# A hybrid attention and RWKV-7 layer: scratch regrouped by four pairs, initial states turned up front

## The chip, the cores and the metric

The kernel runs on one core of one Trainium2 chip. The metric is the device time of one execution in microseconds. A core has five engines with rows of instructions of their own: TensorE (PE, matmuls and transposes), VectorE (DVE), ScalarE (ACT), GpSimd (POOL) and SyncE (SP), which here issues nearly all transfers; 16 DMA engines carry them out. On-chip tiles have 128 partitions.

## What is computed

One inference step of one layer for 256 prompt tokens and 1024 latent tokens of width 1024. One input projection feeds two groups, whose gated outputs go through one output projection:

```python
u = h @ w_in
q, k, v, g_a, u_b, g_b = split(u)
# (A) differential attention, 8 heads of 2 x 64; latent tokens also read 512 cached keys
s = einsum('bqhmd,bkhmd->bhmqk', q, k) * scale
p = softmax(s)
a = p[:, :, 0] - lam * p[:, :, 1]
o_a = rmsnorm(einsum('bhqk,bkhv->bqhv', a, v), subln_g) * (1 - lam_init) * silu(g_a)
# (B) RWKV-7, 16 heads of 64, both directions; r, w, k, v, kk, b come from u_b
def step(S, inp):
    sa = einsum('bhvk,bhk->bhv', S, -kk_t)
    S = S * w_t + sa[..., None] * b_t + v_t[..., None] * k_t
    return S, einsum('bhvk,bhk->bhv', S, r_t)
# prompt: S starts at 0, its final S is an output; latent: S starts at state_rwkv
x = x + gate * (concat([o_a, o_b]) @ w_out)
y = rmsnorm(x, final_g)
```

Outputs are y of both kinds of tokens, the new keys and values of the prompt, and the prompt's final RWKV states (new_s).

## The kernel before

Everything is float32; a projection matmul is done in three passes, the operands split into a high part (hi) and a remainder (lo). The 16 RWKV heads are taken as 8 pairs p of two heads h; d is the direction.

**Projections (0 to about 1223 us).** The 66 weight blocks of 128 columns are taken in a fixed plan. For each, `load_w` (L161) loads the block into one tile w, `split_w` (L167, L170) makes whi and wlo one block ahead of its use, and `chunk` (L337 to L339) runs 24 matmuls for each of three token ranges into a PSUM tile psg. Behind every chunk, the generators of earlier blocks are taken one step on: `b_qk` (L578) makes rotated queries and keys of an attention head, `b_k`/`products`/`gram` the matrices kt, bt, ra of an RWKV pair, and so on. Results go to scratch in DRAM by `spill` (L379), issued on SP: q and k each as two arrays, hi and lo, with one row of 1280 or 1792 tokens for each of 1024 channels. In `b_qk` of a key head the cached keys leave first (L608, L609; 256 KB each), then hi in three pieces through one tile "hi" (L624 to L627), then lo as one store of 640 KB; the last two heads store hi in one piece.

**Mix (from about 1223 us).** The recurrence runs 10 items (two groups of four pairs, each with the prompt and four segments of 256 tokens) of 8 steps (ticks) of 32 tokens, both directions at once; two steps are a part j. `load_part` (L770) brings a part's operands to slots L and R, `load_early` (L792) Bt and Tb for the part after next. `step` (L920) does: 32 matmuls into bank 0 (L933) and their copy into R (L940, ACT), attention work by `fill(0)`, 32 matmuls into bank 1 (L951) and the multiply by the decay on DVE that makes the next state (L962), 32 matmuls for y (L975), the products of Tb and Bt for the next part (`prep` L812, into yb, then `put` L818 on ACT), and more attention by `fill(1)`. PE takes its row in order; the row is made by the tile scheduler from the order of the code, with the step's matmuls raised in priority. `start_item` (L882) turns the states by 64x64 transposes in bank 1 where the prompt's item ends and the latent one begins (L895 to L899). `store_y` (L996), `norm`, `attention` (`load_q` L1064, `load_k` L1072) and `project` (L1309) do the rest; `inverse` (L725) makes Tb's source for each item on POOL.

Names: P = 128, HD = 64, CH = 32 (tokens of a step), HN = 2 (steps of a part), NL = 4 (pairs of a group), T = 1280, NK = 1792, D = 1024.

## Time and profile before

| what | us |
|---|---|
| median of three runs | 2551.7 (2549.16 to 2551.72) |
| the profiled execution | 2542.46 |
| its span | 2540.3 |
| PE busy in the span | 2299.6 (91%) |
| DVE, ACT, POOL busy | 1491.8, 1222.8, 1149.4 |

The profile is of one execution. Its span runs from the first to the last recorded instruction. Busy shares are means over the whole span, and the two halves of the kernel differ much; where a stage is meant, the windows of that stage are read. A DMA share is a mean over 16 engines. [...]

### The profile page before, as it was taken

The numbers are of one execution on the slowest core, as the hardware profiler recorded it, in microseconds if no ns is written. First come the engines' busy times: TensorE is split into PE (matmuls) and PEld (weight loads), VectorE is DVE, ScalarE is ACT, GpSimd is POOL, SyncE is SP. The second block draws the span as 40 slices with busy tenths as digits, with TensorE's granted clock in tenths as the row PEclk, the third lists the DMA queues.
The fourth block names the chain that finished last, engine by engine and source line by source line (L and its number), as shares of the span: only waits on it lengthen the run. The fifth ranks groups of instructions, "written<-read, shape, count | busy, mean of one in ns | idle before, by whom it ended". The sixth has DMA issues, their size and how long they took to land.

```text
span 2540.3 us, 60748 instructions
## 1 busy us (share of the span) xinstructions
PE 2299.6 (91%) x23907; PEld 1880.0 (74%) x23907; DVE 1491.8 (59%) x2950; ACT 1222.8 (48%) x2528; POOL 1149.4 (45%) x1665
## 2 busy tenths in 40 slices
PE   5999999999999999999578887999898889897886
PEld 4888888888888888887467676767686677675675
DVE  5665574646555755433347675666665564666676
ACT  3333444343433444332366676667566565553353
POOL 4244244352433443447554764457485121133274
PEclk9999999999999999999689898999999899998998
DMA  7455656566655565665998897786879889767435
GB/s 246 111 153 135 185 146 171 142 167 164 156 138 160 144 162 138 163 168 158 240 183 166 188 188 167 160 181 148 191 176 224 221 205 223 178 182 217 141 122 183
DMA packets 544893, 437.59 MB, mean 172 GB/s; under 512 B 182151, under 2 KB 481331, under 8 KB 542048
## 3 DMA queue, kind: packets, MB, share of 16 engines
q1 hardware_dynamic: 542512, 427.96, 66.8%
q0 software_dynamic: 2096, 5.75, 1.2%
q8 instruction: 189, 3.10, 0.5%
q14 instruction: 96, 0.79, 0.1%
HBM read 258.69 MB, written 163.86 MB: 166 GB/s over the span
## 4 chain that ended last, share of the span: by engine, by line
PE 53%; DMA 14%; POOL 9%; DVE 8%; SPq 6%; ACT 5%; issue 4%; POOLq 0%; DVEq 0%; ACTq 0%
PE sc L1099 4%; PE po L1144 4%; PE pg L452 3%; PE bank L951 3%; PE pa L1129 2%; PE yb L812 2%; DMA yn<-y 1%; PE pso L1352 1%; PE ptk L456 1%; PE bank L975 1%; PE bank L933 1%; PE psg_v L338 1%; ACT pb L1107 1%; PE psg_v L339 1%; PE psg_v L337 1%
## 5 line engine op out<-in xcount | busy, mean ns | idle before, releaser
L1099 PE MATMUL sc<-ka,q 128*128 128x512 f32 (+1 forms) x832 | 296.0, 447 | 40.1 <-DVE pb L1102 34.3
L1107 ACT ACTIVATE pb<-pb,mn 128x1536 f32<-128x1536 f32 (+1 forms) x160 | 218.3, 1365 | 97.8 <-DVE pb L1102 94.7
L1102 DVE TENSOR_SCALAR_CACHE_REDUCE pb<-sc,mn 128x512 f32<-128x512 f32 x256 | 191.5, 748 | 113.1 <-PE sc L1099 104.8
L1144 PE MATMUL po<-vk,aT 128*128 128x128 f32 x1600 | 233.6, 287 | 3.7 <-ACT aT L1131 3.6
L1144 PEld LDWEIGHTS po<-vk,aT 128*128 128x128 f32 x1600 | 212.9, 198 | 22.7 <-ACT aT L1131 5.7
L484 POOL TENSOR_SCALAR ta<-ta,ka 128x256 f32<-128x256 f32 x80 | 93.8, 1172 | 291.3 <-DVE bk L482 287.0
L738 POOL TENSOR_TENSOR tmp<-aw,tt 128x31 f32<-128x31 f32 (+15 forms) x310 | 165.5, 534 | 120.3 <-DMA aw<-bt 40.0
L459 ACT COPY km<-ptk 64x256 f32<-64x256 f32 x320 | 117.6, 367 | 209.5 <-PE ptk L456 169.8
L1099 PEld LDWEIGHTS sc<-ka,q 128*128 128x128 f32 x832 | 142.1, 202 | 81.7 <-DVE pb L1102 53.1
L740 POOL TENSOR_TENSOR tt<-tt,tmp 128x31 f32<-128x31 f32 (+15 forms) x310 | 183.3, 591 | 19.9
L962 DVE TENSOR_TENSOR R<-bank,wc 64x256 f32<-64x256 f32 x312 | 131.0, 420 | 76.4 <-PE bank L951 73.0
L818 ACT COPY L<-yb 32x384 f32<-32x384 f32 x312 | 146.6, 470 | 56.6 <-PE yb L812 52.8
L453 DVE TENSOR_TENSOR km<-pg,msk 128x512 f32<-128x512 f32 x80 | 55.2, 690 | 200.2 <-PE pg L452 188.4
L1121 DVE SCALAR_TENSOR_TENSOR pb<-pb,cc,pb 128x512 f32<-128x512 f32 (+1 forms) x208 | 170.6, 867 | 2.0
L1102 DVE TENSOR_SCALAR_CACHE_REDUCE pb<-sc 128x512 f32<-128x512 f32 (+1 forms) x160 | 101.3, 635 | 87.0 <-PE sc L1099 72.8
L1129 PE MATMUL pa<-ident,pb 128*128 128x128 f32 x800 | 135.1, 287 | 14.1 <-DVE acc L1346 9.0
L1131 ACT COPY aT<-pa 128x512 f32<-128x512 f32 (+1 forms) x208 | 115.1, 570 | 64.4 <-PE pa L1129 62.3
L940 ACT COPY R<-bank 32x256 f32<-32x256 f32 x320 | 116.1, 363 | 54.1 <-PE bank L933 49.9
L951 PEld LDWEIGHTS bank<-R,L 128*64 128x64 f32 x2560 | 91.9, 150 | 56.4 <-ACT R L940 36.1
L951 PE MATMUL bank<-R,L 128*64 128x64 f32 x2560 | 105.0, 239 | 29.3 <-ACT R L940 29.0
L1129 PEld LDWEIGHTS pa<-ident,pb 128*128 128x128 f32 x800 | 97.9, 145 | 43.6 <-DVE acc L1346 11.6
L1336 POOL TENSOR_TENSOR olo<-of,ohi 128x512 fp32r<-128x512 f32 x30 | 39.0, 1298 | 195.6 <-ACT ohi L1335 120.9
(354 smaller groups left out, 6388.2 us busy)
## 6 DMA issues: line engine op xcount, KB each, us to landing
acc<-acc SPq DMA_DIRECT2D x50, 512.0 KB
ra<-ra SPq DMA_DIRECT2D x160, 128.0 KB
kt<-km SPq DMA_DIRECT2D x160, 128.0 KB
bt<-km SPq DMA_DIRECT2D x160, 128.0 KB
Bt<-bt SPq DMA_DIRECT2D x80, 256.0 KB
L<-kt SPq DMA_DIRECT2D x80, 256.0 KB
L<-ra SPq DMA_DIRECT2D x80, 256.0 KB
R<-vb SPq DMA_DIRECT2D x160, 64.0 KB
```

What stands on the lines that cost most here:

```text
L459: nc.scalar.copy(km[64 * h:64 * h + 64, e:NC:2, 0:HD], pt[64 * e:64 * e + 64, :, 64 * h:64 * h + 64])
L738: e.tensor_tensor(mv, aw[:n, t, t + 1:CH].unsqueeze(2).broadcast_to([n, w, j]), tt[:n, t:t + 1, 0:j].broadcast_to([n, w, j]), op=ALU.mult)
L740: e.tensor_tensor(tt[:n, t + 1:CH, 0:j], tt[:n, t + 1:CH, 0:j], mv, op=ALU.add)
L818: nc.scalar.copy(L[96:128, :, q // 2, q % 2, :, 0:96], pp[32 * q:32 * q + 32, 0:192 * HN].rearrange("p (e c y) -> p e c y", e=2, y=96))
L951: x = nc.tensor.matmul(bank[1][hv(h), o_:o_ + 64], L[:, e, h, d, k, 0:64], R[:, k, d, e, hv(h)], start=True, stop=True, tile_position=(0, ...
L962: hold(nc.vector.tensor_tensor(dst[:, :, :, hv(h)], bank[1][hv(h), 256 * w:256 * w + 256].rearrange("p (d e v) -> p d e v", e=2, d=2), wcs ...
L1099: nc.tensor.matmul(sc, q[:, v, m, qc], ka[:, m, 0:kn], start=(v == 0), stop=(v == 1))
L1102: nc.vector.tensor_scalar(pm[:, c * 512:c * 512 + kn], sc, -0.125, mn[:, c - 1:c] if c else None, op0=ALU.mult, op1=ALU.min, accum_out=mn[ ...
L1107: soon.append(lambda: nc.scalar.activation(v, v, AF.Exp, bias=mn[:, c:c + 1], scale=-1.0, accum_out=B["l"][:, m, B["b"]:B["b"] + 1]))
L1121: nc.vector.scalar_tensor_tensor(a, B["p"][1][:, v], B["cc"], a, op0=ALU.mult, op1=ALU.add)
L1129: nc.tensor.transpose(pt[:, t * P:(t + 1) * P], B["p"][0][:, 512 * c + t * P:512 * c + (t + 1) * P], ident)
L1144: nc.tensor.matmul(po, B["aT"][c][:, t * P:(t + 1) * P], vk[:, t, :], start=(c == 0 and t == 0), stop=(c == last and t == nt - 1))
```

## The change

- The scratch of q becomes one array [H, HD, 2, 2, T] and that of k [H, 2, HD, 2, NK], with hi/lo and the two 64-channel halves as dimensions of their own. The loads of q go from 4 transfers a tile to 2 (64 rows of 4 pieces), those of k from 2 to 1. The stores keep their number; on the DRAM side they are now walked as 2 halves by 64 rows (`r m t -> m r t`).
- ra, kt and bt are grouped by four pairs, not two; a slot has one L and one R, Bt and Tb one tile each. load_part goes from 8 transfers to 4; load_early from 6 to 2, and is issued once in a part, in its second step, behind the second prep and its put; this prep itself moves from behind the y matmuls to behind the first 32 matmuls of that step.
- All initial states are loaded, transposed (16 transposes of 128x64) and stored to scratch s0 among the last projections, and loaded from there at an item's head; the prompt's final state gets a tile of its own, fin, and is turned and stored in the next tick (`new_state`). start_item and load_pairs go.
- The decay multiply is two instructions of 64x512 in place of four of 64x256; the columns of bank 1 are ordered by direction first.
- The rows of oT are reordered so that project loads one tile in one transfer.

SP issues 1827 transfers in place of 2282; DVE has 2378 instructions in place of 2534, ACT 2254 for 2264, PE 16107 for 16139.

SP's row at the first q tile of the projections (hiq is the high part, uq the remainder, km the tile of kt and bt). Before:

```order
77 L379 DMA qhi<-hiq_0_1993 128x512
78 L379 DMA qhi<-hiq_512_1997 128x512
79 L379 DMA qhi<-hiq_1024_2001 128x256
80 L461 DMA kt<-km_1736 32x4x256
81 L463 DMA bt<-km_1736 32x4x256
82 L461 DMA kt<-km_1736 32x4x256
83 L463 DMA bt<-km_1736 32x4x256
84 L379 DMA qlo<-uq_1480 128x1280
85 L161 DMA w_v_2067<-w_in 128x8x128
```

Now:

```order
77 L378 DMA q<-hiq_0_1992 2x64x512
78 L378 DMA q<-hiq_512_1996 2x64x512
79 L460 DMA kt<-km_1735 32x4x256
80 L462 DMA bt<-km_1735 32x4x256
81 L460 DMA kt<-km_1735 32x4x256
82 L462 DMA bt<-km_1735 32x4x256
83 L378 DMA q<-hiq_1024_2000 2x64x256
84 L378 DMA q<-uq_1479 2x64x1280
85 L160 DMA w_v_2066<-w_in 128x8x128
```

The transfers are the same in number, with 2x64 rows in place of 128, and the third piece of hi stands behind kt and bt.

SP's row near the end of the projections: stores of heads 6 and 7, then the first loads of the mix. Before:

```order
713 L161 DMA w_ga_12120<-w_in 128x8x128
714 L585 DMA suk_12029<-uk_11843 16x1024 x8
715 L379 DMA qhi<-hiq_12067 128x1280
716 L379 DMA qlo<-uq_11617 128x1280
717 L161 DMA w_ga_12235<-w_in 128x8x128
718 L379 DMA khi<-hik_12181 128x1280
719 L797 DMA Bt_0_11756<-bt 128x512
720 L802 DMA Tb_0_11758<-td_78 128x1x64 x2
721 L797 DMA Bt_1_11761<-bt 128x512
722 L802 DMA Tb_1_11763<-td_78 128x1x64 x2
723 L776 DMA L_11716<-kt 32x2048
724 L776 DMA L_11736<-kt 32x2048
```

Now:

```order
711 L160 DMA w_ga_12123<-w_in 128x8x128
712 L584 DMA suk_11986<-uk_11818 16x1024 x8
713 L378 DMA q<-hiq_12045 2x64x1280
714 L378 DMA q<-uq_11616 2x64x1280
715 L160 DMA w_ga_12238<-w_in 128x8x128
716 L378 DMA k<-hik_12184 2x64x1280
717 L823 DMA R_11734<-state_rwkv 128x8x64 x2
718 L792 DMA Bt_11753<-bt 128x1024
719 L796 DMA Tb_11755<-td_77 128x1x256
720 L775 DMA L_11715<-kt 32x4096
721 L780 DMA R_11716<-vb 32x2x512 x2
722 L781 DMA L_11715<-ra 64x32x64
```

The two loads of state_rwkv are new behind the last k store; Bt and Tb are one transfer each where there were two and four.

SP's row in the mix, the loads of one part with those around them (y is a step's result, wst a block of the output weights, aw the input of an inverse). Before:

```order
809 L996 DMA y<-ys_2_13181 32x2x256 x4
810 L776 DMA L_11716<-kt 32x2048
811 L776 DMA L_11736<-kt 32x2048
812 L784 DMA R_11717<-vb 32x2x256 x2
813 L785 DMA L_11716<-ra 64x16x64
814 L784 DMA R_11737<-vb 32x2x256 x2
815 L785 DMA L_11736<-ra 64x16x64
816 L1302 DMA wst_3_0_19937<-w_out 128x512
817 L1302 DMA wst_3_1_19954<-w_out 128x512
818 L797 DMA Bt_0_13554<-bt 128x512
819 L802 DMA Tb_0_13556<-td_12531 128x1x64 x2
```

Now:

```order
774 L774 DMA R_11716<-s_68 64x1024
775 L1294 DMA wst_3_0_19537<-w_out 128x512
776 L1294 DMA wst_3_1_19554<-w_out 128x512
777 L729 DMA aw_12970<-bt 16x32x32 x8
778 L792 DMA Bt_13249<-bt 128x1024
779 L989 DMA y<-ys_2_13129 32x2x256 x2
780 L796 DMA Tb_13251<-td_12510 128x1x256
781 L989 DMA y<-ys_2_13129 32x2x256 x2
782 L775 DMA L_11715<-kt 32x4096
783 L780 DMA R_11716<-vb 32x2x512 x2
784 L781 DMA L_11715<-ra 64x32x64
```

The part's eight loads became four, Bt and Tb of all four pairs stand ahead of them in one piece, and the state's load from scratch (s, L774) leads the item.

The diff, cut to its core (the old start_item, load_pairs, load_part and the old loops of step are in the listing above):

```diff
-    scratch("qhi", [D, T])
-    scratch("qlo", [D, T])
-    scratch("khi", [D, NK])
-    scratch("klo", [D, NK])
+    scratch("q", [H, HD, 2, 2, T])
+    scratch("k", [H, 2, HD, 2, NK])
...
-    scratch("ra", [H // 2, 5, NF, HD, 2, 2, 2, HN * HD])
-    scratch("kt", [H // 2, 5, NF, CH, 2, 2, 2, HN * P])
-    scratch("bt", [H // 2, 5, NF, 2, 2, CH, 2, HN * P])
+    scratch("ra", [H // NL, 5, NF, HD, NL, 2, 2, HN * HD])
+    scratch("kt", [H // NL, 5, NF, CH, NL, 2, 2, HN * P])
+    scratch("bt", [H // NL, 5, NF, 2, 2, CH, NL, HN * P])
...
+    scratch("s0", [HD, heads // NL, 2, NL, P])
...
-            rows = slice(h * P, (h + 1) * P)
+            dq = lambda v, c: (s["q"][h, :, v, :, c] if which == "q" else s["k"][h, v, :, :, c]).rearrange("r m t -> m r t")
...
-                nc.sync.dma_start(s["khi"][rows, 0:PAST], ch)
-                nc.sync.dma_start(s["klo"][rows, 0:PAST], cv)
+                nc.sync.dma_start(dq(0, slice(0, PAST)), ch)
+                nc.sync.dma_start(dq(1, slice(0, PAST)), cv)
...
-                spill(s[which + "hi"][rows, off:off + T], hi)
-                spill(s[which + "lo"][rows, off:off + T], u[:, 0:T])
+                spill(dq(0, slice(off, off + T)), hi)
+                spill(dq(1, slice(off, off + T)), u[:, 0:T])
                 return
             for n0, n in CHUNKS:
                 hi = ap.tile([P, 512], F32, tag="hi", name=f"hi{which}{h}_{n0}", bufs=1)[:, :n]
                 nc.scalar.copy(hi.bitcast(F32R), u[:, n0:n0 + n])
                 nc.vector.tensor_tensor(u[:, n0:n0 + n].bitcast(F32R), u[:, n0:n0 + n], hi, op=ALU.subtract)
-                spill(s[which + "hi"][rows, off + n0:off + n0 + n], hi)
-            spill(s[which + "lo"][rows, off:off + T], u[:, 0:T])
+                spill(dq(0, slice(off + n0, off + n0 + n)), hi)
+            spill(dq(1, slice(off, off + T)), u[:, 0:T])
...
+        L, R = slots[j % 2]
+        if f == 0 and sg == -1:
+            nc.gpsimd.memset(R[0:64, 0], 0.0)
+        if f == 0 and sg == 0:
+            nc.sync.dma_start(R[0:64, 0].rearrange("k d x v -> k (d x v)"), s["s0"][:, p0 // NL].rearrange("k d x v -> k (d x v)"))
+        nc.sync.dma_start(L[64:96].rearrange("r x h d c y -> r (x h d c y)"),
+                          s["kt"][p0 // NL, sg + 1, f].rearrange("r x h d y -> r (x h d y)"))
+        for d in range(2):
+            t0 = tok0(sg, d) + CH * HN * (NF - 1 - f if d else f)
+            src = s["vb"][t0:t0 + CH * HN, p0 * P:(p0 + NL) * P].rearrange("(c t) y -> t c y", t=CH)
+            nc.sync.dma_start(R[64:96, :, d].rearrange("t c x v -> t c (x v)"), src[:, ::-1] if d else src)
+        nc.sync.dma_start(L[0:64, :, :, :, :, 64:128].rearrange("r x h d c y -> r (x h d c) y"),
+                          s["ra"][p0 // NL, sg + 1, f].rearrange("r x h d (c y) -> r (x h d c) y", y=HD))
...
+    def load_early(j):
...
+        Bt = cp.tile([P, NL, HN, P], F32, tag="Bt", name=f"Bt{j}")
+        nc.sync.dma_start(Bt.rearrange("r x c y -> r (x c y)"),
+                          s["bt"][p0 // NL, sg + 1, f].rearrange("h d r x y -> (h d r) (x y)"))
+        Tb = cp.tile([P, HN, NL, CH], F32, tag="Tb", name=f"Tb{j}")
+        src = tds[m].rearrange("t (f q u) s -> f q t (u s)", f=NF, q=4)
+        nc.sync.dma_start(Tb.rearrange("t c x s -> t (c x s)"), src[f])
+        early[j] = (Bt, Tb)
...
 
-    for w in duos:
-        load_early(0, w)
+    flat = lambda n: slots[n][1].rearrange("p c d x v -> p (c d x v)")
+    raw = flat(1)[:, 0:2 * heads * HD].rearrange("p (d x k) -> p d x k", d=2, k=HD)
+    for d in range(2):
+        nc.sync.dma_start(raw[:, d], i["state_rwkv"][0, 0, d, 0:2 * heads].rearrange("(x h) v k -> (h v) x k", h=2))
+    load_early(0)
+    yield
+    yield
+    for g in range(heads // NL):
+        for d in range(2):
+            px = psm.tile([P, 512], F32, tag="psm", name=f"ps0{g}{d}")
+            for x in range(NL):
+                nc.tensor.transpose(px[0:HD, P * x:P * x + P], raw[:, d, NL * g + x, :], ident)
+            c = 512 * (2 * g + d)
+            nc.scalar.copy(flat(0)[0:HD, c:c + 512], px[0:HD])
+    nc.sync.dma_start(s["s0"].rearrange("k g d x v -> k (g d x v)"), flat(0)[0:HD, 0:heads * 2 * P])
+    yield
     for j in range(2):
         load_part(j)
         yield
@@ -833,8 +841,7 @@
         pp = psm.tile([P, 512], F32, tag="psm", name=f"pp{w}")
         prep(0, w, pp, [])
         put(0, w, pp)
-    for w in duos:
-        load_early(1, w)
+    load_early(1)
...
+    def new_state(m):
...
+        fin = fins.pop(m)
+        px = pst.tile([P, 512], F32, tag="pt", name=f"pfin{m}")
+        for d in range(2):
+            for x in range(NL):
+                c = HD * (NL * d + x)
+                nc.tensor.transpose(px[:, c:c + HD], fin[0:HD, d, x, :], ident[0:64, 0:64])
+        fo = wk.tile([P, 2, 256], F32, tag="bv", name=f"fo{m}", bufs=2)
+        nc.scalar.copy(fo.rearrange("p d y -> p (d y)"), px)
+        for d in range(2):
+            nc.sync.dma_start(o["new_s"][0, 0, d, 2 * p0:2 * (p0 + NL)].rearrange("(x h) v k -> (h v) x k", h=2),
+                              fo[:, d].rearrange("p (x k) -> p x k", k=HD))
...
+                                                 R[0:96, k, d, 2 * w + e, hv(h)], start=True, stop=True, tile_position=(0, u))
                             held(x, chain)
+            if k == HN - 1 and j + 1 < n_part:
+                prep(j + 1, 1, yb, chain)
             for w in duos:
-                R = slots[w, j % 2][1]
                 for h in range(2):
                     u = 64 * w + 32 * h
-                    hold(nc.scalar.copy(R[96:128, k, :, :, hv(h)],
+                    hold(nc.scalar.copy(R[96:128, k, :, 2 * w:2 * w + 2, hv(h)],
                                         bank[0][u:u + 32, 0:256].rearrange("p (d e v) -> p d e v", d=2, e=2)))
+        if k == HN - 1 and j + 1 < n_part:
+            put(j + 1, 1, yb)
+            if j + 2 < n_part:
+                load_early(j + 2)
...
+            for x_ in range(NL):
+                for d in range(2):
+                    for h in range(2):
+                        o_ = 256 * d + 64 * x_
+                        x = nc.tensor.matmul(bank[1][hv(h), o_:o_ + 64], L[:, x_, h, d, k, 0:64],
+                                             R[:, k, d, x_, hv(h)], start=True, stop=True, tile_position=(0, 64 * h))
+                        held(x, chain)
+            if k < HN - 1:
+                dst = R[0:64, k + 1]
+            elif f == NF - 1 and sg == 3:
+                dst = None
+            elif f == NF - 1 and sg == -1:
+                fins[m] = wk.tile([HD, 2, NL, P], F32, tag="st", name=f"fin{m}")
+                dst = fins[m]
+            else:
+                dst = slots[(j + 1) % 2][1][0:64, 0]
+            for h in range(2):
+                if dst is not None:
+                    hold(nc.vector.tensor_tensor(dst[:, :, :, hv(h)], bank[1][hv(h), :].rearrange("p (d x v) -> p d x v", d=2, x=NL),
+                                                 wcs[p0][hv(h), :, sg + 1, :, c:c + 1].rearrange("p x d o -> p d x o").broadcast_to([HD, 2, NL, HD]),
+                                                 op=ALU.mult))
...
-            if j + 1 < n_part:
-                prep(j + 1, k, yb, chain)
+            for x_ in range(NL):
+                o_ = 256 + 64 * x_
+                for h in range(2):
+                    for d in range(2):
+                        q = 64 * d + 32 * h
+                        x = nc.tensor.matmul(bank[0][q:q + 32, o_:o_ + 64], L[:, x_, h, d, k, 64:96], R[:, k, d, x_, hv(h)],
+                                             start=True, stop=True, tile_position=(0, q))
+                        follow(x, chain)
+            if k == 0 and j + 1 < n_part:
+                prep(j + 1, 0, yb, chain)
             nc.scalar.copy(ysb[m, g][:, k], bank[0][:, 256:512].rearrange("p (x v) -> p x v", x=NL))
-        if j + 1 < n_part:
-            put(j + 1, k, yb)
-        if j + 2 < n_part:
-            load_early(j + 2, k)
+        if k == 0 and j + 1 < n_part:
+            put(j + 1, 0, yb)
...
     def load_q(h, g):
         n0, n = QG[g]
         q = ap.tile([P, 2, 2, n], F32, tag=f"q{g}", name=f"q_{h}_{g}")
-        for v, w in enumerate(("qhi", "qlo")):
-            src = s[w][h * P:(h + 1) * P, n0:n0 + n].rearrange("(m r) t -> r m t", m=2)
-            for e in range(2):
-                nc.sync.dma_start(q[64 * e:64 * e + 64, v], src)
+        for e in range(2):
+            nc.sync.dma_start(q[64 * e:64 * e + 64].rearrange("r v m t -> r (v m) t"),
+                              s["q"][h, :, :, :, n0:n0 + n].rearrange("r v m t -> r (v m) t"))
         qs[h, g] = q
 
     def load_k(h, g):
         k0, n = KC[g]
         z = "s" if g == 3 else ""
         ka = ap.tile([P, 2, n], F32, tag="ka" + z, name=f"ka_{h}_{g}", bufs=1 if g == 3 else 4)
-        for e, w in enumerate(("khi", "klo")):
-            nc.sync.dma_start(ka[64 * e:64 * e + 64],
-                              s[w][h * P:(h + 1) * P, k0:k0 + n].rearrange("(m r) k -> r m k", m=2))
+        nc.sync.dma_start(ka, s["k"][h, :, :, :, k0:k0 + n].rearrange("e r m k -> (e r) m k"))
```

## Rows read from the trace of the kernel before

**Rows 1.** The page: PE in 40 slices, tenths; the chain that ended last, by engine.
```profile
PE   5999999999999999999578887999898889897886
...
PE 53%; DMA 14%; POOL 9%; DVE 8%; SPq 6%; ACT 5%; issue 4%; POOLq 0%; DVEq 0%; ACTq 0%
```

**Rows 2.** Windows: length, then busy us (instructions) by engine, clock, DMA share, GB/s.
```profile
180.00:620.00 440.00, 433.15 (x3656) 367.35 (x3657) 257.62 (x398) 177.43 (x340) 176.88 (x197) 1.00 0.60 158
620.00:1190.00 570.00, 562.46 (x4103) 476.57 (x4102) 310.65 (x467) 215.28 (x412) 263.41 (x281) 1.00 0.60 157
...
1235.00:1600.00 365.00, 290.90 (x4836) 233.66 (x4837) 220.85 (x530) 234.81 (x517) 218.32 (x403) 0.88 0.87 183
```

**Rows 3.** PE's waits from 180 to 1190: total us, times, longest.
```profile
PE pg L452 <- POOL bk L486: 14.7, 12, 2.5
```

**Rows 4.** DMA view, 178.6 to 181, one store: packets, MB, engines' share.
```profile
q1 hardware_dynamic: 144, 0.26, 29.3%
```

**Rows 5.** DMA view, 1201.2 to 1202.3, Tb loads: busy tenths in slices; share.
```profile
DMA  0001000001123221333233323211112222233233
...
q1 hardware_dynamic: 211, 0.05, 21.0%
```

**Rows 6.** Timeline: start, us, instruction; load, split and first matmul of one weight.
```profile
700.18 0.39 SPq L161 DMA_DIRECT2D w_v<-w_in  x1
...
708.70 1.04 ACT L167 CAST whi_v<-w_v 128x1024 fp32r<-128x1024 f32 x1 [2.21 <-PE psg_ak L338]
...
725.71 0.40 PE L337 MATMUL psg_v<-hhi,whi_v 128*128 128x512 f32 x1
```

**Rows 7.** Timeline of SP: first and last of head 0's six k stores.
```profile
239.94 0.53 SPq L608 DMA_DIRECT2D khi<-ch  x1
...
255.69 0.54 SPq L379 DMA_DIRECT2D klo<-uk  x1
```

**Rows 8.** Timeline of SP: first and last of nine stores, heads 6 and 7.
```profile
1142.81 0.35 SPq L379 DMA_DIRECT2D qhi<-hiq  x1
...
1182.09 0.32 SPq L379 DMA_DIRECT2D khi<-hik  x1
```

**Rows 9.** Window around the end of the projections.
```profile
1140.00:1223.00 83.00, 76.91 (x441) 65.79 (x440) 30.56 (x59) 17.30 (x35) 52.50 (x58) 0.92 0.69 165
```

**Rows 10.** By line: issues and matmuls; min/median/max ns, first and last start.
```profile
L797 SPq DMA_DIRECT2D Bt<-bt x80: 325/414/2463, 1182.5 to 2192.6; - x80
...
L802 SPq DMA_DIRECT2D Tb<-td x160: 507/545/1511, 1199.9 to 2193.6; - x160
...
L812 PE MATMUL pp<-Bt,Tb x64: 332/362/365, 1202.6 to 1206.9; 32*32 32x96 f32 x64
```

**Rows 11.** Tile hik: what ended its engine's idle time; us, times.
```profile
  DMA khi<-ch: 20.4, 6
  DMA khi<-hik: 15.3, 8
```

**Rows 12.** Pieces of the chain: a store, then two loads behind 1235.
```profile
574.63 2.88 DMA khi<-ch
...
1243.95 8.61 DMA ka<-khi
1252.57 8.95 DMA q<-qhi
```

**Rows 13.** PE's waits from 1235 to 2420.
```profile
PE yb L812 <- DMA Tb<-td: 10.2, 4, 6.0
...
PE bank L933 <- DVE R L962: 4.7, 6, 1.8
...
PE bank L933 <- DMA Tb<-td: 3.1, 1, 3.1
```

**Rows 14.** The page's groups: count, then busy us, mean ns, idle before, releaser.
```profile
L962 DVE TENSOR_TENSOR R<-bank,wc 64x256 f32<-64x256 f32 x312 | 131.0, 420 | 76.4 <-PE bank L951 73.0
...
L453 DVE TENSOR_TENSOR km<-pg,msk 128x512 f32<-128x512 f32 x80 | 55.2, 690 | 200.2 <-PE pg L452 188.4
```

157 lines of the change are left out of this document (33 added, 124 removed).

## The prediction

> **What bounds the kernel now.** I read the page's slices first, then the windows by stage, then PE's waits, then the transfers. The slices show two halves: up to about slice 19 PE stands at 9 tenths or more, behind it at 7 to 9 [rows 1]. The windows say the same in microseconds: from 180 to 1190 PE works 995.6 of 1010 us at a granted clock of 1.00, while from 1235 to 1600 it works 290.9 of 365 and the DMA engines are busy 0.87 of the time [rows 2]. So the projections are bound by TensorE, and a transfer there is free as long as it lands before it is wanted: the only wait of weight that PE has in these 1010 us is 14.7 us on POOL [rows 3]. The mix (recurrence, attention, output projection) is bound by several things in turn; in the chain that ended last, over the whole span, DMA has 14% and SP's issuing 6% [rows 1]. The reader should keep in mind that the DMA share is a mean over 16 engines: 0.60 in the projections [rows 2] leaves room only if a transfer is spread over all of them.
>
> **Part 1, the stores of q and k (projections).** The 72 stores of q and k, 25.2 MB, keep their bytes and their number, but their destination is now walked as 2 halves of a head by 64 rows, where it was 128 rows. How many engines take part in such a transfer is to be read from two places. One store qhi<-hiq of 256 KB with 128 rows, alone in its window, takes 29.3% of 16 engines in 2.4 us, 11.25 us of engine time or 0.70 us on each of 16 [rows 4]. The loads of Tb have a source walked as 4 outermost pieces (by 32 rows) and a destination of 128 partitions; while they alone run, the slices stand at 2 to 3 tenths, that is 4 of 16 engines [rows 5]. So the outermost count of the DRAM side, 4, set the number of engines although the other side has 128 rows. With a count of 2 I take 2 engines: 256 KB then take 5.6 us on each of two engines. From the rows alone the bounds are 4 engines (2.8 us) and 16 (0.70 us, nothing changes); 2 is what the row with the nearest form gives by its own pattern. [...]
>
> One head's k tile is 1792 KB (seven times 256: 39 us on the two engines), its q tile 1280 KB (five: 28 us). Eight heads give 540 us on each of two engines, where 67 us were. Everything else is at most the share 0.60 of 1010 us [rows 2], and at least what its bytes take at the rate of that one store (0.26 MB in 11.25 us, 23.3 GB/s an engine, against 158/16 = 9.9 GB/s: 0.42). Less the stores' own 67 us and plus 540 us, the two engines have 0.89 to 1.07 of the time to do: near full, on average. What decides is the burst. Head 0's six k stores go out within 16 us [rows 7]; half the two engines' time is free meanwhile, so some 31 us of stores (39 - 8) stand ahead of the next weight, all of whose rows cross those engines too. A weight load has a lead of 25.5 us from its issue to its first matmul; the split begins 8.5 us behind the issue and needs about 3 us [rows 6], so it can be 14 to 17 us late before PE stands still. A load right behind a k burst makes PE wait some 31 - 16 = 15 us, behind a q burst (28 us in 8: 24 left) 8 us; but loads come some 16 us apart, so on average one comes 8 us behind the burst's end, when 4 us have drained: 11 + 4 = 15 us a head if none is hidden, 90 for six heads. PE's own standing still gives the engines time, and bursts that no load follows closely cost nothing; I take a third, **+30** (0 to +90). The single tile hi is a second way: ACT's copy into it already sits idle 20.4 + 15.3 us behind these stores [rows 11], when one lands in 2.9 us [rows 12]; with landings three times as long that is 70 us more of ACT waiting, which PE feels only through a PSUM tile that isn't emptied. It is in the upper end.
>
> The last two heads are surer. Nine of their stores, 4992 KB, go out between 1142.8 and 1182.1 [rows 8]: 110 us on two engines. The loads of the first part follow at once, Bt at 1182.5, and PE uses them at 1202.6 [rows 10]; R<-state_rwkv, whose transposes now stand in PE's row, is in the same place (front, second piece of the order). Up to then there are 60 us of engine time, of which the rest of the traffic wants 0.42 to 0.69 [rows 9], less the 14 us that these stores had: 11 to 27 us. 110 + 11 - 60 = 61 and 110 + 27 - 60 = 77 us late. Part of that is the last weights' wait (and so also their lead), and head 7's remaining k stores (another 25 us of two engines) meet a stage with the DMA engines at 0.87. I take **+65** (45 to 80). Part 1 is +95 (45 to 165, with hi's 70 as the mishap beyond: up to 200).
>
> **Part 2, fewer transfers (mix).** SP issues 1827 transfers where it issued 2282; about 450 of the 455 fall behind 1190. The issues cost 0.41 us (Bt) to 0.55 us (Tb) [rows 10], so SP loses about 220 us of issuing, but only what lies on the chain counts: SP's 6% of 2540 us is 152 us for all 2282 [rows 1], and a fifth of it is **-30** (0 to -80, half of SP's chain). The bytes stay, so DMA's 14% stay.
>
> **Part 3, the initial states.** The 64 transposes of 64x64 and 16 ACT copies at the heads of two items leave the recurrence, which waited there; 16 new transposes and 4 copies stand among the last projections, and 8 with one copy behind each prompt item. No row above prices them; the nearest is the multiply of the copies' shape, 0.42 us [rows 14]: 16 copies are at most 7 us on the chain, and the 20 instructions up front at most 8 us if nothing covers them (PE and ACT have other work beside them there). I take **-5** (-7 to +8); the wait for their load is in part 1.
>
> **Part 4, the decay multiply.** 312 at 420 ns become 156 of 64x512; the nearest row, 128x512 at 690 ns [rows 14], makes 108 us of 131. Off the path that saves nothing. On it, the first half of the state is ready at 0.69 instead of 0.42 and the last at 1.38 instead of 0.84 us behind the last matmul: +0.54 us in 78 ticks is +42 at most. PE waited for this multiply 4.7 us in six places [rows 13], so **+5** (-10 to +42).
>
> **Part 5, Bt and Tb for all four pairs at once.** They are issued after the second prep of a part and used by the first prep of the next but one: the lead falls from two steps to little more than one (some 11 us). Loads at this end take 8.6 and 9.0 us [rows 12], and behind load_part's large transfers in SP's row more. PE's waits for Tb now are 10.2 + 3.1 us [rows 13]; a prep that waits stands in PE's row in front of the next state matmul, so ACT's put and all of the next step wait with it. I take the waits doubled, **+10** (0 to +80, 2 us in each of 39 parts). The oT and aw changes are a few issues, counted in part 2.
>
> **Sum.** +95 - 30 - 5 + 5 + 10 = +75. The profiled execution took 2542.5 us (span 2540.3), the median of the runs is 2551.7, 9.2 above. Since parts 1 and 2 are each taken in full although late loads give SP slack to hide in, I round down by 10: 2542.5 + 65 + 9.2 = 2617.
>
> **Rivals.** (a) The stores cost nothing: either a count of 2 doesn't confine them, or later loads pass them on the two engines instead of queueing. For it: nothing in this trace has a count of 2, and PE's slack of 14 to 17 us is real. Against: rows 5, and loads at the ramp land 8.6 and 9.0 us after they become first, against 2.9 us for a store in the projections [rows 12], which looks like a queue. Then only parts 2 to 5 are left: 2542.5 - 20 + 9.2 = 2532, with part 2's upper end 2480: faster, not slower. [...] (b) The two engines are the bound from the first store on (1.07 of the time, rows 2 and 4) and hi holds up ACT: +165 for part 1, 2542.5 + 165 - 20 + 9.2 = 2697. It decides if the rest of the traffic really occupies 0.60 and not the 0.42 of its bytes. (c) The halved lead of Bt and Tb turns into a wait in every part: +80 in place of +10, 2617 + 70 = 2687. It decides where SP's queue holds them longer than a step. (d) The issues saved are off the chain (part 2 is 0): 2647.
>
> **How the numbers follow.** Forecast with (d) as its upper neighbour 0.51, (a) 0.17, (b) 0.20, (c) 0.12. A measurement of this kernel tells about 0.2%, 5 us, from no change. Faster holds most of (a), 0.15, and 0.03 of the forecast's low end (45 for part 1 with 80 saved): 0.18; same 0.04; slower 0.78. The range reaches from the upper half of (a), 2532, to (b) with its bound of 200 for part 1: 2542.5 + 200 - 20 + 9.2 = 2732.
>
> **What would show it.** Right: PE's waits from 180 to 1190 name DMA w<-w_in or ACT whi many times, some tens of us in all; the stretch from 1140 to the first pp matmul is 60 us longer; the DMA slices drop to 1 or 2 tenths where only a q or k store runs. Mix (first bank matmul to the end) is 10 to 40 us shorter. Wrong: PE's busy share up to 1190 stays at 98% (rival a); the mix stage is longer and PE waits for Tb or Bt in tens of places (c).

## The result: 13% slower, and the profile after

The changed kernel takes 2895.3 us (median, 2880.9 to 2901.9); the kernel before, on the same chip, 2550.4. The ratio is 1.135 with a 95% interval of 1.130 to 1.140. I had forecast 2617 and a range of 2532 to 2732: the direction was right, the size was not.

The page of the kernel after shows where: three rows of its slices (PE's busy tenths, the granted clock in tenths of full, the DMA engines' mean share), which answer to [rows 1].

```profile
PE   6978779896887987986644689889989998998896
...
PEclk9998899997998999998877899999989999799898
DMA  7354545553543644554237988978687977857534
```

PE now stands at 6 to 9 tenths in the first half as well, and the clock beside it falls below 9 again and again. The windows say how much belongs to which part; columns as in [rows 2]. After:

```profile
180.00:1190.00 1010.00, 837.76 (x6423) 705.00 (x6422) 455.06 (x726) 320.82 (x619) 317.05 (x360) 0.92 0.48 125
1190.00:1549.00 359.00, 242.28 (x1543) 203.47 (x1541) 97.73 (x167) 77.14 (x154) 120.58 (x131) 0.84 0.45 111
1549.00:2583.00 1034.00, 921.74 (x13213) 700.97 (x13214) 571.75 (x1296) 633.58 (x1383) 476.80 (x887) 0.92 0.80 182
2583.00:2890.00 307.00, 248.91 (x1332) 197.91 (x1330) 199.51 (x447) 124.66 (x259) 141.61 (x184) 0.93 0.55 175
```

and, for the mix before (first state matmul to last, and the rest):

```profile
1228.00:2234.00 1006.00, 874.40 (x13252) 688.68 (x13245) 607.34 (x1453) 634.73 (x1397) 488.69 (x892) 0.92 0.82 188
2234.00:2540.00 306.00, 250.89 (x1322) 199.58 (x1320) 204.37 (x443) 124.89 (x257) 144.96 (x183) 0.92 0.55 173
```

The first state matmul (bank<-R,L into bank 0) started at 1227.1 us before and starts at 1549.5 now. So the projections with their handover are 322 us longer, and the mix, 1313 us before and 1340 now, is 27 longer. In the first of these rows PE works 838 of 1010 us where it worked 996 [rows 2], and the DMA engines are *less* busy on average: 0.48 for 0.60.

**The stores are on two engines.** The DMA view of 181.5 to 189, in which one store of q with 256 KB is issued and nothing else (columns as in [rows 4, 5]; the second row is what each slice moved):

```profile
DMA  1011130012011111111111111111111000000000
GB/s 22 0 55 33 44 44 0 11 55 22 22 44 44 55 33 55 44 55 55 44 55 55 44 55 55 44 55 55 44 55 55 33 0 0 0 0 0 0 0 0
...
q1 hardware_dynamic: 124, 0.25, 10.2%
```

One tenth is what two of sixteen engines make (0.125). 10.2% of 16 engines in 7.5 us are 12.2 us of engine time, 6.1 us on each of two; 0.70 us on each of sixteen is what the same store took before [rows 4]. I had put 5.6.

**Who waits.** PE's waits from 180 to the first state matmul, the five longest; before, up to 1190, there was one row of 14.7 us and next to nothing else [rows 3]:

```profile
PE pg L451 <- POOL bk L485: 93.7, 24, 16.5
PE z L417 <- DVE km L452: 55.5, 6, 12.1
PE psg_av L336 <- ACT uv L347: 25.7, 1, 25.7
PE pg L451 <- DVE bk L482: 22.0, 6, 12.5
PE psg_ga L336 <- ACT uv L347: 14.9, 1, 14.9
```

None of these five names a transfer (the longest behind them that does is 13.6 us for w_ada), so I looked one step further back, at the tiles behind them. What ended the idle time in front of the instructions on tile km (the one tile of kt and bt, written by DVE and ACT, read by their stores), before:

```profile
  PE pg L452: 188.4, 55
  PE ptk L456: 169.8, 61
```

and after:

```profile
  DMA bt<-km: 186.4, 18
  PE ptk L455: 169.9, 43
```

and the same for hik after, which answers to [rows 11]:

```profile
  DMA k<-hik: 94.5, 12
  DMA k<-ch: 49.1, 6
```

Tile km did not wait for its stores at all before (no such row); now DVE and ACT stand 186.4 us in front of it because bt<-km, which is not itself walked as 2 halves, has not landed. Releasers are inferred from semaphores, and no row of the profile tells the 16 engines apart; my reading is that bt<-km has rows on the two engines too, and that these stand behind the stores'. SP too is held up while it issues; its timeline behind the first q tile:

```profile
197.49 0.49 SPq L378 DMA_DIRECT2D q<-uq  x1
198.07 0.61 SPq L160 DMA_DIRECT2D w_v<-w_in  x1
198.74 11.94 SPq L643 DMA_DIRECT2D w_ada<-w_ada  x1
210.78 3.85 SPq L460 DMA_DIRECT2D kt<-km  x1
214.68 0.43 SPq L462 DMA_DIRECT2D bt<-km  x1
```

The issue of w_ada takes 11.94 us and that of kt 3.85, where such issues took 0.4 us [rows 6, 10].

### The profile page after: what moved, and what is told of

It is laid out like the page before. It is cut to its first block, busy times and chain, and to the rows that moved or that the text cites. A ratio compares the mean times of both kernels' runs of the same rounds, so it can differ in the third digit from the quotient of the medians.

```text
span 2889.6 us, 59844 instructions
## 1 busy us (share of the span) xinstructions
PE 2402.2 (83%) x23875; PEld 1931.3 (67%) x23875; DVE 1424.4 (49%) x2794; ACT 1218.8 (42%) x2518; POOL 1120.2 (39%) x1655
## 5 line engine op out<-in xcount | busy, mean ns | idle before, releaser
L1098 ACT ACTIVATE pb<-pb,mn 128x1536 f32<-128x1536 f32 (+1 forms) x160 | 218.2, 1364 | 80.9 <-DVE pb L1093 79.4
L1135 PE MATMUL po<-vk,aT 128*128 128x128 f32 x1600 | 244.6, 291 | 6.0 <-ACT aT L1122 5.9
L451 PE MATMUL pg<-ra,bk 64*64 64x64 f32 x2560 | 101.8, 235 | 115.7 <-POOL bk L485 93.7
L451 PEld LDWEIGHTS pg<-ra,bk 64*64 64x64 f32 x2560 | 90.3, 147 | 140.1 <-POOL bk L485 102.6
L1120 PE MATMUL pa<-ident,pb 128*128 128x128 f32 x800 | 138.4, 291 | 32.4 <-ACT aT L1122 15.9
L1112 DVE SCALAR_TENSOR_TENSOR pb<-pb,cc,pb 128x512 f32<-128x512 f32 (+1 forms) x208 | 161.3, 822 | 2.0
L806 PE MATMUL yb<-Bt,Tb 32*32 32x96 f32 x2496 | 110.2, 260 | 27.8 <-DMA Tb<-td 11.4
```

The lines of the kernel that those rows point to most:

```text
L451: nc.tensor.matmul(pg[hs, c, :], bk[hs, c, :], ra[hs, c, :], start=True, stop=True)
L806: follow(nc.tensor.matmul(pp[g, n:n + 96], Tb[g, c, 2 * w + e, :], Bt[g, 2 * w + e, c, 0:96], start=True, stop=True, tile_position=(32 * q ...
L1098: soon.append(lambda: nc.scalar.activation(v, v, AF.Exp, bias=mn[:, c:c + 1], scale=-1.0, accum_out=B["l"][:, m, B["b"]:B["b"] + 1]))
L1112: nc.vector.scalar_tensor_tensor(a, B["p"][1][:, v], B["cc"], a, op0=ALU.mult, op1=ALU.add)
L1120: nc.tensor.transpose(pt[:, t * P:(t + 1) * P], B["p"][0][:, 512 * c + t * P:512 * c + (t + 1) * P], ident)
L1135: nc.tensor.matmul(po, B["aT"][c][:, t * P:(t + 1) * P], vk[:, t, :], start=(c == 0 and t == 0), stop=(c == last and t == nt - 1))
```

## The experiments

All kernels below were profiled too; "first state" is the start of the first bank<-R,L matmul in that profile, "mix" the rest of its span. Ratios are against runs of the kernel before on the same chip. Each profile is one execution, and single executions of the kernel before lie between 2530.6 and 2575.2 us on these chips, so that a difference of 20 us between two mixes says little by itself.

| kernel | median us | ratio (95%) | first state | mix |
|---|---|---|---|---|
| before | 2550.4 | 1 | 1227 | 1313 |
| after | 2895.3 | 1.135 (1.130 to 1.140) | 1549 | 1340 |
| e1_halves | 2617.2 | 1.027 (1.023 to 1.031) | 1249 | 1375 |
| e_hi_two | 2755.4 | 1.082 (1.077 to 1.087) | 1404 | 1344 |
| e_lo_two | 2747.9 | 1.079 (1.074 to 1.083) | 1406 | 1343 |
| e_before_two | 2880.2 | 1.128 (1.123 to 1.134) | 1548 | 1332 |
| e_before_four | 2703.4 | 1.062 (1.055 to 1.069) | 1392 | 1303 |
| e3_after_actq | 2932.7 | 1.152 (1.147 to 1.158) | 1547 | 1390 |
| e2_layout | 2612.2 | 1.027 (1.023 to 1.031) | 1240 | 1374 |
| e2_attn_only | 2547.8 | 1.000 (0.998 to 1.002) | 1231 | 1317 |
| e2_early | 2614.7 | 1.028 (1.024 to 1.032) | 1235 | 1378 |
| e2_dve4 | 2622.5 | 1.031 (1.027 to 1.034) | 1236 | 1383 |
| e3_layout_1000 | 2535.9 | 0.995 (0.992 to 0.998) | 1234 | 1305 |
| e3_before_200 | 2602.5 | 1.022 (1.017 to 1.027) | 1230 | 1369 |
| e4_before_1000 | 2521.2 | 0.986 (0.982 to 0.990) | 1232 | 1288 |
| e4_layout_1500 | 2527.0 | 0.988 (0.984 to 0.992) | 1236 | 1288 |

### Projections: is it the stores, and how does the loss come about?

**e1_halves** undoes the walk by two alone:

```diff
+        def spill2(dq, v, c, t):
+            for m in range(2):
+                nc.sync.dma_start(dq(v, c)[m], t[64 * m:64 * m + 64])
...
-                spill(dq(0, slice(off, off + T)), hi)
+                spill2(dq, 0, slice(off, off + T), hi)
```

(and so for the other stores of q and k).

> The changed kernel, each of the 72 stores of q and k issued as two of 64 rows, so that 64 is the outermost count on both sides; the layout of the scratch and all else is kept. Theory A (stores on two engines cost the projections their 321 us: first state matmul at 1549 now, 1228 before): first state matmul back at 1220 to 1250, total about 2575 if the mix keeps the 28 us that it is longer by. Rival B (the regrouped kt, bt and ra, the states' turning up front or the new order cost it): first state matmul stays behind 1450, total over 2800.

First state matmul at 1249: 300 of the 322 us are back. Theory A holds for the projections, rival B falls. The total, 2617, is 42 above what I expected, since the mix became still longer; that is taken up below.

**e_before_two** makes the same walk the only edit to the kernel before:

```diff
+        def two(dst):
+            return dst.rearrange("(r m) t -> m r t", m=2)
...
-                spill(s[which + "hi"][rows, off:off + T], hi)
+                spill(two(s[which + "hi"][rows, off:off + T]), hi)
...
-            src = s[w][h * P:(h + 1) * P, n0:n0 + n].rearrange("(m r) t -> r m t", m=2)
+            src = s[w][h * P:(h + 1) * P, n0:n0 + n].rearrange("(r m) t -> r m t", m=2)
```

> The kernel before with one edit: the stores of q and k are walked on the DRAM side as 2 by 64 rows (channel 64m + r in row 2r + m), and the loads read the rows accordingly; nothing else of the change. Theory A: total 2550 + 300, 2790 to 2900, first state matmul at 1500 to 1560. Rival B: 2540 to 2600.

First state matmul at 1548, total 2880: one edit makes nearly the whole of the result, with the same number of transfers and the same bytes as before. What stops tile km in it:

```profile
  DMA bt<-km: 198.3, 19
```

**e_hi_two, e_lo_two** confine one half of the bytes each, starting from e1_halves:

```diff
+        def spill2(dq, v, c, t):
+            if v == 0:
+                return spill(dq(v, c), t)
+            for m in range(2):
+                nc.sync.dma_start(dq(v, c)[m], t[64 * m:64 * m + 64])
```

(e_hi_two; e_lo_two has `v == 1`).

> As e1_halves, but the hi parts (half of the bytes) are stored in one piece by 2 x 64 rows, the lo parts as two of 64 rows. If the carrier is the single tile hi, for which ACT and DVE wait at every piece: most of the loss, about 2800. If it is the two engines' work and the queue in front of them: half the work is mostly hidden, 2600 to 2680, and the same as e_lo_two.

> The mirror image: the lo parts by 2 x 64 rows in one piece, the hi parts as two stores of 64 rows. If the single tile hi is the carrier: 2575 to 2600, little above e1_halves. If the two engines' work and the queue are: 2600 to 2680, the same as e_hi_two.

Both lose the same, as the second theory says, but far more than it says: 155 and 157 us of first state against e1_halves, where both together lose 300. The loss is in proportion to the bytes, although the wait is in another place each time. Of e_hi_two:

```profile
  DMA bt<-km: 72.0, 15
```

```profile
  DMA k<-hik: 79.4, 12
  DMA k<-ch: 47.7, 6
```

and of e_lo_two:

```profile
  DMA bt<-km: 157.9, 12
```

```profile
  DMA k<-hik: 33.5, 10
  DMA k<-ch: 17.4, 6
```

With hi confined, ACT waits for the hi tile (79.4 + 47.7 us for the keys alone) and km for 72.0; with lo confined, km takes 157.9 and hi 33.5 + 17.4. So no one of the shallow tiles is *the* cause: whichever is there first waits.

**e_before_four** walks the stores as 4 by 32 rows (m=4 in `two`), everything else as in e_before_two.

> As e_before_two, but the DRAM side of the stores is walked as 4 by 32 rows; the loads still read as in e_before_two, so that the channels of q and k arrive in another order and the scores are others (nothing of the work is left out). By the loss in proportion to the stores' time on each engine (e_hi_two and e_lo_two lost half as much as both): half of 335, total 2700 to 2730. By my prediction's picture of bursts that drain between two loads: nearly all hidden, 2550 to 2590.

The loads then bring the channels in another order, so the scores are others; no work is left out. That four engines carry a store shows in a window in which one alone is issued (181.5 to 186, columns as above): 2 to 3 tenths, where it was 1.

```profile
DMA  3123022222322222222211000000000000000000
...
q1 hardware_dynamic: 110, 0.22, 13.5%
```

First state matmul at 1392, 165 us late, where two engines made 321: a ratio of 0.51 at half the time on each engine. The proportion holds again; the picture of bursts that drain between two loads does not.

**e3_after_actq** leaves the stores on two engines but issues them from ACT:

```diff
-                spill(dq(0, slice(off + n0, off + n0 + n)), hi)
+                nc.scalar.dma_start(dq(0, slice(off + n0, off + n0 + n)), hi)
```

> The changed kernel with one edit: the stores of q and k, still walked as 2 by 64 rows, are issued by ACT in place of SP, so that weight loads and the stores of kt, bt and ra no longer stand behind them in SP's own row and queue. Theory Q (what the projections lose is the queue behind the stores: other transfers on the two engines, and SP held up while it issues): most of the 321 us comes back, total 2600 to 2700. Rival C (the two engines simply cannot do the work in the time, whoever issues): 2850 to 2900, or more, since ACT is now held up too.

First state matmul at 1547: nothing comes back, so theory Q falls as far as SP's own row and queue go. What stops tile km:

```profile
  DMA bt<-km: 171.8, 16
```

The other transfers are as late as before although the stores stand in another engine's row and queue, and although SP's issues are shorter again (the longest of kt<-km takes 3.4 us, 11.9 in the changed kernel). SP's long issues were a symptom; what is left as short is the time of the two engines. The mix of this kernel, 1390, is 50 longer than the changed kernel's; I did not trace that.

### Mix: why is it longer, not shorter?

**e2_layout** keeps all of the change but lays q and k out as [head, hi/lo, half, 64, tokens]: each store is one transfer of 128 rows, q still loads by 2 transfers a tile, k by 2.

```diff
-    scratch("q", [H, HD, 2, 2, T])
-    scratch("k", [H, 2, HD, 2, NK])
+    scratch("q", [H, 2, 2, HD, T])
+    scratch("k", [H, 2, 2, HD, NK])
...
-            dq = lambda v, c: (s["q"][h, :, v, :, c] if which == "q" else s["k"][h, v, :, :, c]).rearrange("r m t -> m r t")
+            dq = lambda v, c: s[which][h, v, :, :, c].rearrange("m r t -> (m r) t")
...
-                              s["q"][h, :, :, :, n0:n0 + n].rearrange("r v m t -> r (v m) t"))
+                              s["q"][h, :, :, :, n0:n0 + n].rearrange("v m r t -> r (v m) t"))
...
-        nc.sync.dma_start(ka, s["k"][h, :, :, :, k0:k0 + n].rearrange("e r m k -> (e r) m k"))
+        for e in range(2):
+            nc.sync.dma_start(ka[64 * e:64 * e + 64], s["k"][h, e, :, :, k0:k0 + n].rearrange("m r k -> r m k"))
```

> The changed kernel with another layout of the same scratch: q and k as [head, hi/lo, half, 64, tokens], so that each store is one transfer of 128 rows again; q is still loaded by 2 transfers a tile, k by 2 in place of 1. All else of the change stays. If the stores' walk is all that hurt the projections: first state matmul at 1225 to 1240 (e1_halves 1249, where the split stores added 72 issues), total 2570 to 2600, since the mix was 27 to 62 us longer in every form of the change so far. Rival: the up-front states or the regrouped kt, bt, ra also cost the projections; then the first state matmul stays at 1249 or later.

First state matmul at 1240, 13 us behind the kernel before; the up-front states and the order around them can cost no more than that. The mix is 60 us longer than before, 1374, and the total of 2612 lies above the 2600 that I had allowed. The next three look for the part that does it.

**e2_attn_only** takes from e2_layout the q and k scratch and from the change the oT order, on top of the kernel before; the recurrence is untouched.

> The kernel before with only the attention side and the output side of the change: q and k in the layout of e2_layout (q loads 2 in place of 4), oT reordered and loaded by one transfer. The recurrence, its loads, its states and its order are those of before. If the mix's 27 to 62 us come from the recurrence's part of the change: 2525 to 2545, a little under the kernel before. If they come from this part: 2570 to 2600.

No difference (0.998 to 1.002). The mix's loss comes with the recurrence's part of the change; and 88 transfers fewer in the attention and the output projection (48 of q, 40 of oT) bring no gain that can be measured.

**e2_early** gives Bt and Tb back their halves, their lead of two steps and their place behind the y matmuls:

```diff
-    def load_early(j):
+    def load_early(j, w):
...
-            if k == HN - 1 and j + 1 < n_part:
-                prep(j + 1, 1, yb, chain)
...
-            if k == 0 and j + 1 < n_part:
-                prep(j + 1, 0, yb, chain)
+            if j + 1 < n_part:
+                prep(j + 1, k, yb, chain)
...
+            load_early(j + 2, k)
```

> e2_layout with one edit undone: Bt and Tb in halves with tiles of their own, issued half in each step two steps ahead, and both preps behind the y matmuls, as in the kernel before. If the shorter lead and the moved prep make the mix longer: 30 to 50 us under e2_layout. If the cause is elsewhere: within 10 us of e2_layout.

2614.7 beside 2612.2: no difference. PE's wait for Tb does shrink, from the first of these rows (e2_layout, first state matmul to the end) to the second (e2_early), without any gain:

```profile
PE yb L806 <- DMA Tb<-td: 32.4, 6, 8.6
```

```profile
PE yb L809 <- DMA Tb<-td: 7.3, 4, 3.7
```

**e2_dve4** splits the decay multiply into four again:

```diff
+            for w in duos if dst is not None else ():
+                xs_ = slice(2 * w, 2 * w + 2)
-                    hold(nc.vector.tensor_tensor(dst[:, :, :, hv(h)], ...
+                    hold(nc.vector.tensor_tensor(dst[:, :, xs_, hv(h)], ...
```

> e2_layout with the decay multiply as four instructions of 64x256 again, in the new order of bank 1's columns. If the longer chain on DVE behind the last state matmul (1.38 in place of 0.84 us a step by the rows of before) makes the mix longer: 20 to 40 us under e2_layout. If it is covered: within 10 us.

2622.5 beside 2612.2, not less: the longer chain on DVE is covered.

So none of the waits I had named makes the mix longer. The windows show what does. From the first to the last state matmul PE worked 874 us before, 922 after (rows above), and in e2_layout:

```profile
1240.00:2308.00 1068.00, 948.83 (x13187) 708.88 (x13191) 583.31 (x1295) 631.44 (x1380) 485.61 (x886) 0.92 0.79 176
```

949 us: PE is *busier*, at the same granted clock of 0.92, with nearly the same matmuls. What differs is their order. I counted, in PE's row of each built program from the first state matmul on, the places where a matmul has other operands than the one ahead of it, by the names of the tiles with their numbers left out (so it is a change of the kind of matmul; with the numbers, the kernel before changes the more often, 3193 times to 2536): 2388 before, 2515 after, 2556 in e1_halves, 2594 in e2_layout, 2609 in e2_early, 2457 in e2_attn_only. The scheduler breaks the step's groups (state, y, Tb by Bt) up more, with attention's matmuls in between.

In the trace of the kernel before, 514 of 1042 us of PE's work in the mix (in time at the full clock) are such first matmuls, 0.215 us each from the end of the one ahead; the other 12,184 take 0.043 each. These two means mix shapes. Like for like, in plain time, a matmul of R and L takes 0.197 us behind another kind and 0.023 behind its own, one of ka and q 0.332 and 0.257: 0.17 and 0.08 us more. From the kernel before to e2_layout, counted in the traces in the same way, the first matmuls grow from 541 to 623 us (more of them, and 0.248 us each in place of 0.235), and the others fall from 585 to 574: all that PE is busier by lies in the first ones.

That is a theory (F) with a price, 0.22 us a change, and two kernels put it to the proof in opposite directions, by one number each: the priority with which the scheduler raises a step's matmuls (HPC = HPY = 500 in both kernels).

**e3_layout_1000** and **e3_before_200**:

```diff
-HPC = 500
+HPC = 1000          # e3_layout_1000, on e2_layout; 200 in e3_before_200, on the kernel before
-HPY = 500
+HPY = 1000
```

> e2_layout with the priority of a step's matmuls raised from 500 to 1000 (HPC and HPY), so that the scheduler breaks them up less with attention's: in PE's row of the mix the operand changes 2222 times from one matmul to the next, 2594 in e2_layout, 2388 in the kernel before. Theory F (the mix of the changed kernel is longer since PE's row is more broken up, about 0.22 us at each change of operands): 2612 less 372 x 0.22 = 80, about 2530. Rival W (PE is longer because of waits for Tb, Bt and L): 2600 or more, as the order does not bring the loads earlier.

> The kernel before with the same priority lowered from 500 to 200: 2632 changes of operands in PE's row of the mix in place of 2388, and nothing else of the change. Theory F: 2547 + 244 x 0.22 = 54, about 2600. Rival W: within 15 us of 2547.

Theory F called 2530 and 2600; measured were 2535.9 and 2602.5. By these two, a change of operands is worth (2612.2 - 2535.9)/372 = 0.21 us (0.19 if each is taken against the kernel before on its own chip) and (2602.5 - 2542.5)/244 = 0.25 us. A priority moves the whole order, and a raised one could also gain by letting the chain of states wait less. But it is PE's busy time that moves. The recurrence and the rest, e3_layout_1000 and then e3_before_200:

```profile
1235.00:2180.00 945.00, 811.66 (x12945) 645.35 (x12935) 544.74 (x1223) 609.28 (x1340) 473.71 (x862) 0.92 0.87 192
2180.00:2540.00 360.00, 299.58 (x1588) 240.24 (x1586) 230.18 (x518) 145.85 (x300) 154.79 (x208) 0.92 0.53 168
```

```profile
1230.00:2323.00 1093.00, 989.00 (x13469) 747.04 (x13470) 626.28 (x1509) 655.60 (x1433) 504.34 (x917) 0.91 0.77 178
2323.00:2598.00 275.00, 220.32 (x1124) 175.13 (x1124) 180.26 (x391) 104.70 (x220) 125.70 (x156) 0.89 0.54 172
```

PE is busy for 1111 us of the mix in e3_layout_1000, 1197 in e2_layout; for 1209 in e3_before_200, 1125 in the kernel before. e3_layout_1000 is also a little faster than the kernel before, 0.995 (0.992 to 0.998).

**e4_before_1000** and **e4_layout_1500** ask what is left of the change's merit at an equal priority, and how far the order's effect goes (HPC = HPY = 1000 on the kernel before, 1500 on e2_layout).

> The kernel before with the priority of a step's matmuls raised from 500 to 1000: 2128 changes of operands in PE's row of the mix in place of 2388, nothing of the change. By theory F alone, 0.22 us a change: 2545 - 57 = 2488. If the mended change is worth something of its own at an equal order of PE: this one comes out above e3_layout_1000 (2536). If the gain of e3_layout_1000 was the order alone: below it, 2490 to 2520, and the fewer, larger transfers of the recurrence cost rather than save.

> e2_layout with that priority at 1500: 2051 changes of operands in place of 2222 at 1000 and 2594 at 500. Theory F: 2536 - 38 = 2498. If attention's work, pushed behind the recurrence, is missed there as cover (the stretch behind the last state matmul was 360 us at 1000, 305 at 500): 2530 to 2560.

The kernel before with the raised priority takes 2521.2 us, the fastest of all and 1.4% under the kernel before (0.982 to 0.990). It is below e3_layout_1000, so the gain there came with the order. The two orders are not equal: this one has 94 changes fewer, 21 us at 0.22. It is 15 us faster by the medians and 26 by each one's distance to the kernel before on its own chip, so the fewer, larger transfers of the recurrence saved nothing that shows. Neither kernel came down in full proportion (2488 and 2498 by theory F); 2527.0 lies between theory F and the 2530 to 2560 called for missing cover. In e4_layout_1500 the window from the first to the last state matmul, and the one behind it:

```profile
1236.00:2102.00 866.00, 716.36 (x12680) 586.43 (x12679) 507.67 (x1136) 583.67 (x1289) 465.96 (x847) 0.92 0.91 197
2102.00:2524.00 422.00, 350.62 (x1872) 281.09 (x1864) 266.29 (x606) 170.80 (x350) 163.28 (x223) 0.93 0.55 167
```

The recurrence is 202 us shorter than in e2_layout, but 422 us stand behind it, where e2_layout has 305: attention that was pushed aside is done later, with less beside it to fill PE.

The price of a change is therefore no constant. e2_attn_only changes 69 times more than the kernel before, 15 us at 0.22, and its mix is 4 us longer; e1_halves 168 times more, 37 us, and its mix is 62 longer; e4_before_1000 260 times less, 57 us, and it is 32 faster than the kernel before on its chip. The count tells the direction in the large, not the size.

## Why the prediction was right and wrong

**Part 1, two engines (right).** That an outermost count of 2 on the DRAM side confines a store to two engines, read from the loads of Tb, is shown by the window of one store (10.2% of 16 engines in 7.5 us), and by four engines costing half of two (165 us of first state matmul, and 321). The price of 5.6 us for 256 KB was 6.1. The slices of one store stand at 1 tenth here, with a count of 2, and at 2 to 3 in e_before_four, with a count of 4.

**Part 1, the handover (the size right, by luck; the path wrong).** From the q store of head 6 (1142.81 before [rows 8], 1389.55 now) to the first state matmul it was 84 us before and is 160 now: +76, where I had +65 (45 to 80). I had the loads of the first part come late. Of them PE waits for R<-state_rwkv alone, 6.3 us; 53.7 us of its waits there (25.7 and 14.9 above, and 13.1) are for ACT's copies of the last projections into uv and uk:

```profile
PE psg_av L336 <- ACT uk L347: 13.1, 1, 13.1
PE ps L831 <- DMA R<-state_rwkv: 6.3, 1, 6.3
```

and what ACT waits for in front of the copies into uv:

```profile
ACT uv L347 <- DMA suk<-uk: 38.0, 1, 38.0
ACT uv L347 <- DMA q<-uq: 27.0, 1, 27.0
```

So it is again a tile that transfers must leave first (u). The granted clock was 0.77 in this stretch, 0.91 before.

**Part 1, heads 0 to 5 (wrong; this is the step that failed).** The same store comes 247 us later; I had +30 (0 to +90). Two things in that step were wrong. First, who feels the queue: I followed the weights, which have a lead of 25 us, and hi, and left out km, whose stores had never made anyone wait. It has one buffer as hi has; 186 us of idle time end with its store. "PE feels only through a PSUM tile that isn't emptied", I wrote of hi and put it in the upper end alone, but PE takes its row in order (in the trace of the kernel before, its 1957 groups of matmuls with one output tile come in the order of the program), and it stands at pg for POOL (93.7 us) and DVE (22.0) and at z for DVE (55.5). The sign that I had named for being right, PE's waits for w<-w_in or whi in many places, did not show: up to the first state matmul PE waits 1.5 us for whi, although between 180 and 1389 ACT stood 30.7 us in front of whi_v until w_v<-w_in landed. The lead hid that, as I had said it would. Second, the draining: I let PE's slack hide what follows a burst by more than 16 us. The runs show a loss in proportion to the time that the stores take on each engine, at half the bytes (155 and 157 us of 300) and at twice the engines (165 of 321) alike: 300 us against e1_halves, of some 96 x 6.1 = 586 us, about half. Why half is not shown. That the two engines would be 0.89 to 1.07 full was the better sum, and I turned away from it; rival (b), +165, was the nearest case and still half of what came.

**The clock (not in the sum).** The projections ran at a granted clock of 1.00; now it is 0.92 and 0.84 in the two windows above. Up to the first state matmul the trace's clock records stand at half of full for 290 us in all, in 32 stretches, and for 25 us, in 5, before. PE had waited ahead of each of the 32: it was busy for 27 to 78% of the last 7 us (so from 501.4 to 508.4, for 2.3 us at 1.00; then come 10.2 us at 0.50). That the waits bring the lower clock about is not shown. The lower clock is part of the loss above, not beside it: PE's busy time up to the first state matmul grew by 58 us (1173 to 1232, from the records of matmuls), the other 264 us are idle time.

**Part 2, fewer transfers (wrong).** -30 was forecast from SP's share of the chain; e2_attn_only and e4_before_1000 against e3_layout_1000 show no gain. The mix was to be 10 to 40 us shorter and is 27 longer. A likely reason, not shown: SP's share of a chain was time in which SP was the last of several, with the next right behind. A gain of some 15 us could be hidden in e2_attn_only, if its 69 more changes of operands cost 0.22 us each.

**Parts 3 to 5 (harmless, as said).** The up-front states: at most 13 us (e2_layout). The decay multiply: not worse than before (e2_dve4). The shorter lead of Tb: 32.4 us of waits in e2_layout in place of 13.3 [rows 13], and no effect on the total (e2_early); rival (c) did not come about.

**What I did not see.** The order of PE's row in the mix. I compared SP's rows and the places that the diff moves, and took PE's row as unchanged elsewhere. It had 127 more changes of operands; at 0.22 us that is 28 us, and the mix grew by 27. With a price that is no constant this agreement is luck in part; what the runs show is that the order moves PE's busy time by this much and more. Why the scheduler breaks the groups up more in the recurrence's new form is open: neither the place of prep nor the multiply does it alone, and the merged tiles and the states were not tried apart. Nor is the count the whole of it: e2_layout is 20 us above what it gives (2612 against 2547 + 206 x 0.22 = 2592), and that rest was not traced to a line.

## What to carry to other kernels

Look at the outermost count on the DRAM side of a transfer before regrouping a scratch for better loads: here the stores paid (6.1 us on each of two engines for 256 KB, where it was 0.70 on each of sixteen), and the price fell on other transfers too (186.4 us in front of km, ended by bt<-km), in proportion to the time the stores take on each engine (155 to 165 us at half of it, 300 to 321 at the whole), not only on late loads. Before hoping that slack hides it, list every tile with one buffer that a store must leave, also those that no wait names yet. And where a scheduler makes a row, count how often the row changes operands before and after; here that order went far to decide the mix, and one number in the old kernel was worth more than the whole change.

## What was unexpected of the hardware

- Two of sixteen engines moved 55 GB/s at most when they alone ran (the slices of the window above), and while stores ran there SP's issues of other transfers took up to 11.94 us in place of 0.4. Issuing the stores from ACT left the other transfers as late (172 us at km in place of 186).
- The mean DMA share fell, 0.60 to 0.48, while transfers became the bound: a mean over 16 engines hides two that are nearly full (0.89 to 1.07 by the prediction's sum; no row shows them by themselves).
- A small fp32 matmul (R, L) behind one of another kind takes 0.17 us more of PE than behind its own in the kernel before (0.197 and 0.023), which shows as PE being busy, not as a wait. Moving the priority alone away from 500 made 0.12 (e4_before_1000) to 0.25 us (e3_before_200) a change.
